# Where seven block products replace eight: heads gain them, two projections lose them

## The chip, the core and the metric

One NeuronCore of a Trainium2 chip runs the whole block as one launch. The metric is the device time of that launch in microseconds (us). The kernel before takes 2250.86 us, median of 3 runs (2249.49 to 2253.15).

## What is computed

One residual block on 256 tokens with D = 2048, 8 retention heads (key width 256, value width 512) and a feed-forward width of 5632, all in float32:

```
h = RMSNorm(x)
[cb|cc|cv | q|k|v|g | gate_conv|gate_ret] = h @ w_in
y_conv = (cb * causal_dwconv3(cc * cv)) @ w_conv_out
y_ret  = (silu(g) * GroupNorm(Retention(rotary q, rotary k, v))) @ w_ret_out
x += (sigmoid(gate_conv) * y_conv + sigmoid(gate_ret) * y_ret) @ w_o
x += SwiGLU(RMSNorm(x))                      # w_ffn_in: 2048 x 11264, w_ffn_out: 5632 x 2048
x += sigmoid(RMSNorm(x) @ w_ple_gate) * (p @ w_ple_proj)
out = RMSNorm(x)
```

## The kernel before, in words

**Split products.** Every float32 operand is written as a high part of type fp32r and the rest, also fp32r. A product of a 128 x 128 stationary block of activations and a 128 x 512 moving block of weights is then three matmuls (hi·hi, hi·lo, lo·hi): `thrice`, lines 227 to 229, and `products`, lines 353 to 355. A chunk of weights comes by DMA into a raw buffer (3 of them, `raw_pool`); ScalarE (ACT) casts it to the high part and VectorE (DVE) subtracts to get the low part (`halves`, lines 333 and 334). These parts lie in `part_pool`, six tiles, so three plain chunks are in flight. Weights stream through once; the 256 tokens are two halves t of 128.

**Two kinds of product.** `project` makes 512 columns of output for both token halves from 16 row blocks of the weights: 96 matmuls into two PSUM banks. `product_group` makes two such column blocks c1 and c2 at once, over 8 pairs of row blocks. A plain pair is a 2 x 2 by 2 x 2 block product with 8 block products, that is 24 matmuls. In a *fast* pair (a table such as `FAST3` says which) seven block products do, 21 matmuls; for these, four sums of the weight blocks are made on DVE (lines 261, 262, 264, 265) with their own casts and low parts (lines 263, 266 and 268), and four sums of the activation blocks, the *stationary forms*, are made once by `further_forms` (lines 208 to 222) for all column blocks that use them. The products of a group run in seven PSUM banks out of eight up to the last fast pair; then DVE joins the banks (lines 293 to 297) and at the end adds what came later (line 302). `FAST3` has fast pairs 1, 3 and 5; `FAST4` has 1, 3, 4 and 6.

**Order of the work.** Heads 0 to 4, each as gate projection g (with its SiLU), q and k together with the rotation on DVE (lines 573 to 587), and v, then scores, values, group norm, and transposes into yrT; then `ret_out(0)` over the first four heads; heads 5 to 7; the convolution's groups `conv_cv` (cc and cv of one column block) and `conv_b` (cb of two), with `ret_out(1)` after the first; four `gate` groups for gate_conv and gate_ret; two groups `co` (w_conv_out) and two groups `wo` (w_o); eleven groups `f` (w_ffn_in), with `fo` (w_ffn_out) woven in from the third on; the embedding gate `pg` and the end. Small steps such as transposes are put off with `later(n, fn)`, which runs fn after n more chunks of weights. All groups from the convolution to w_ffn_in are `product_group`s with FAST3, or FAST4 in w_ffn_in.

**Engines.** Tile pools and a scheduler turn this into one fixed order for each engine, and semaphores keep data apart. On each engine instructions run in that order.

## Time and profile before

| what | value |
|---|---|
| median of 3 runs | 2250.86 us |
| the profiled execution's own time | 2248.99 us |
| its span | 2247.2 us |
| TensorE (PE) busy, matmuls | 2186.1 us, 97%, 9796 matmuls |
| weight loads (PEld) busy | 1781.5 us, 79% |
| DVE busy | 1712.8 us, 76% |
| ACT busy | 1061.1 us, 47% |
| HBM traffic | 190 GB/s over the span |
| mean granted TensorE clock | 0.994 |

A matmul's row in the profile lasts longer than the time to the next one's start, since matmuls are pipelined; how fast PE runs is read from the distance of the starts, or from the number of matmuls in a stretch. The share of DVE differs strongly between stages, so the stages are looked at apart.

### The profile page before, as it was taken

The numbers are of one execution on the slowest core, as the hardware profiler recorded it, in microseconds if no ns is written. First come the engines' busy times: TensorE is split into PE (matmuls) and PEld (weight loads), VectorE is DVE, ScalarE is ACT, GpSimd is POOL, SyncE is SP. The second block draws the span as 40 slices with busy tenths as digits, with TensorE's granted clock in tenths as the row PEclk, the third lists the DMA queues.
The fourth block names the chain that finished last, engine by engine and source line by source line (L and its number), as shares of the span: only waits on it lengthen the run. The fifth ranks groups of instructions, "written<-read, shape, count | busy, mean of one in ns | idle before, by whom it ended". The sixth has DMA issues, their size and how long they took to land.

```text
span 2247.2 us, 25045 instructions
## 1 busy us (share of the span) xinstructions
PE 2186.1 (97%) x9796; PEld 1781.5 (79%) x9796; DVE 1712.8 (76%) x1797; ACT 1061.1 (47%) x967; POOL 9.4 (0%) x19
## 2 busy tenths in 40 slices
...
GB/s 260 187 190 171 181 182 177 218 207 176 184 150 195 253 205 172 161 199 184 224 197 200 197 189 173 150 185 189 225 188 180 175 189 206 187 225 192 187 186 133
DMA packets 235126, 428.47 MB, mean 191 GB/s; under 512 B 11392, under 2 KB 46336, under 8 KB 235008
## 3 DMA queue, kind: packets, MB, share of 16 engines
...
HBM read 420.54 MB, written 6.29 MB: 190 GB/s over the span
## 4 chain that ended last, share of the span: by engine, by line
PE 80%; DVE 10%; ACT 5%; DMA 3%; issue 2%; SPq 0%; ACTq 0%; DVEq 0%; POOLq 0%
PE f_p L228 5%; PE f_p L229 5%; PE f_p L227 5%; PE g_ps L353 3%; PE g_ps L355 3%; PE fo_ps L353 3%; PE fo_ps L355 3%; PE g_ps L354 3%; PE fo_ps L354 3%; PE v_ps L353 3%; PE qk_ps L353 3%; PE v_ps L355 3%; PE v_ps L354 3%; PE ro_ps L227 3%; PE qk_ps L354 3%; PE ro_ps L229 3%
## 5 line engine op out<-in xcount | busy, mean ns | idle before, releaser
L334 DVE TENSOR_TENSOR f_b_lo<-f_raw,f_b_hi 128x2048 fp32r<-128x2048 f32 (+1 forms) x88 | 177.3, 2023 | 61.3 <-ACT f_b_hi L333 61.3
L333 ACT CAST f_b_hi<-f_raw 128x2048 fp32r<-128x2048 f32 (+1 forms) x88 | 148.8, 1693 | 88.3 <-PE fo_ps L354 48.9
L228 PE MATMUL f_p<-f_b_lo,h2T_hi 128*128 128x512 f32 x374 | 146.7, 392 | 1.9 <-DVE f_b_lo L334 1.7
L229 PE MATMUL f_p<-f_b_hi,h2T_lo 128*128 128x512 f32 x374 | 146.0, 390 | 0.0
L227 PE MATMUL f_p<-f_b_hi,h2T_hi 128*128 128x512 f32 x374 | 135.8, 396 | 4.7 <-ACT f_b_hi L333 4.6
L354 PE MATMUL fo_ps<-fo_lo,aT_hi 128*128 128x512 f32 x352 | 138.0, 392 | 0.0
L353 PE MATMUL fo_ps<-fo_hi,aT_hi 128*128 128x512 f32 x352 | 137.2, 394 | 0.0
L355 PE MATMUL fo_ps<-fo_hi,aT_lo 128*128 128x512 f32 x352 | 137.1, 390 | 0.0
L334 DVE TENSOR_TENSOR ro_lo<-ro_raw,ro_hi 128x2048 fp32r<-128x2048 f32 x32 | 73.3, 2291 | 74.7 <-ACT ro_hi L333 74.7
L263 ACT CAST f_t_hi<-f_raw 128x1024 fp32r<-128x1024 f32 x44 | 46.4, 1054 | 167.3 <-DVE f_raw L262 75.5
L334 DVE TENSOR_TENSOR qk_lo<-qk_raw,qk_hi 128x2048 fp32r<-128x2048 f32 x32 | 73.3, 2292 | 60.8 <-ACT qk_hi L333 60.8
L334 DVE TENSOR_TENSOR g_lo<-g_raw,g_hi 128x2048 fp32r<-128x2048 f32 (+1 forms) x36 | 73.9, 2053 | 59.2 <-ACT g_hi L333 59.1
L268 DVE TENSOR_TENSOR f_t_lo<-f_raw,f_t_hi 128x1024 fp32r<-128x1024 f32 x88 | 106.4, 1221 | 16.3 <-ACT f_t_hi L266 8.9
L334 DVE TENSOR_TENSOR v_lo<-v_raw,v_hi 128x2048 fp32r<-128x2048 f32 x32 | 73.3, 2290 | 59.4 <-ACT v_hi L333 59.4
L333 ACT CAST fo_hi<-fo_raw 128x2048 fp32r<-128x2048 f32 x44 | 84.2, 1914 | 68.9 <-PE fo_ps L354 41.0
L333 ACT CAST v_hi<-v_raw 128x2048 fp32r<-128x2048 f32 x32 | 61.2, 1913 | 111.9 <-PE qk_ps L354 86.0
L334 DVE TENSOR_TENSOR fo_lo<-fo_raw,fo_hi 128x2048 fp32r<-128x2048 f32 x44 | 100.6, 2287 | 15.9 <-ACT fo_hi L333 15.9
L333 ACT CAST ro_hi<-ro_raw 128x2048 fp32r<-128x2048 f32 x32 | 61.2, 1912 | 97.7 <-PE ro_ps L228 80.0
L333 ACT CAST qk_hi<-qk_raw 128x2048 fp32r<-128x2048 f32 x32 | 61.1, 1909 | 92.6 <-PE g_ps L354 73.5
L353 PE MATMUL g_ps<-g_hi,hT_hi 128*128 128x512 f32 x256 | 100.7, 395 | 4.2 <-ACT hT_hi L171 4.2
L354 PE MATMUL g_ps<-g_lo,hT_hi 128*128 128x512 f32 x256 | 100.5, 393 | 0.0
L353 PE MATMUL v_ps<-v_hi,hT_hi 128*128 128x512 f32 x256 | 100.5, 393 | 0.0
...
## 6 DMA issues: line engine op xcount, KB each, us to landing
...
```

What stands on the lines that cost most here:

```text
L227: nc.tensor.matmul(out=ps, lhsT=xh, rhs=wh, start=first, stop=False)
L228: nc.tensor.matmul(out=ps, lhsT=xh, rhs=wl, start=False, stop=False)
L229: nc.tensor.matmul(out=ps, lhsT=xl, rhs=wh, start=False, stop=last)
L263: nc.scalar.copy(out=hi[:, 0:2, :], in_=raw[:, 0:2, :])
L268: tt(out=lo[:, js, :], in0=raw[:, js, :], in1=hi[:, js, :].bitcast(F32), op=ALU.subtract)
L333: last_copy[0] = nc.scalar.copy(out=hi[:, :n, :], in_=src)
L334: nc.vector.tensor_tensor(out=lo[:, :n, :], in0=src, in1=hi[:, :n, :].bitcast(F32), op=ALU.subtract)
L353: nc.tensor.matmul(out=ps, lhsT=xh[:, ts], rhs=wh, start=first, stop=False)
L354: nc.tensor.matmul(out=ps, lhsT=xh[:, ts], rhs=wl, start=False, stop=False)
L355: nc.tensor.matmul(out=ps, lhsT=xl[:, ts], rhs=wh, start=False, stop=last)
```

## The change

A second table, `FAST2`, has two fast pairs (1 and 3). Heads 1 to 7 project g and v in one `product_group` with FAST2 instead of two `project`s, after q and k; their scores are made in that group, and the group norm's last step goes from DVE to ACT. The stationary forms of h are asked for in head 0. The convolution's groups use FAST2 instead of FAST3, and the first of them is now a plain group for cb (column blocks 0 and 1). The gate groups keep FAST3. w_conv_out and w_o become plain (`plain_group`, 192 matmuls, four banks), and so their stationary forms go. w_ffn_in uses FAST2 for its first two groups and FAST4 after that; the source of h2's forms is written by ACT from PSUM and not added up on DVE. The matmuls become 9826, the DVE instructions 1692 (1797 before), and ACT's remain 932 in the program.

```diff
+FAST2 = (False, True, False, True, False, False, False, False)
...
             pt = transposed(src, j0, f"{name}_t{j0}")
+            a = form_source(f"{name}_{j0}") if forms is not None and any(forms[1][len(forms[0]) :]) else None
...
+                    if a is not None:
+                        nc.scalar.activation(out=a[:, j, :], in_=pt[:, j, :], func=AF.Copy, scale=g)
+            if forms is not None:
+                further_forms(a, *forms, f"{name}_{j0}")
...
+    def plain_group(lhs, w, k0, c1, c2, name):
+
+        ps = [[bank(f"{name}_ps{c}{t}") for t in range(NT)] for c in range(2)]
+        n = D // P
+        for k in range(0, n, 2):
+            ws = halves(load_pair(w, k0 + k, c1, c2, f"{name}_{k}"), f"{name}_{k}")
+            for j in range(2):
+                xh, xl = lhs[k0 + k + j]
+                for c in range(2):
+                    for t, ts in enumerate((t1, t2)):
+                        thrice(ps[c][t], (xh[:, ts], xl[:, ts]), ws[2 * c + j], k == j == 0, k + j == n - 1)
+            group_done()
+        return ps
...
-        for t in range(NT):
-            nc.vector.tensor_scalar(
-                out=on[:, t, :],
-                in0=o_ps[t],
...
+        for t in range(NT):
+            nc.scalar.activation(
+                out=on[:, t, :], in_=o_ps[t], func=AF.Identity, scale=rstd[:, t : t + 1], bias=shift[:, t : t + 1]
             )
...
+    def head(h):
+        mask = small.tile([P, 3 * P], F32, tag="mask", name=f"mask{h}")
+        nc.sync.dma_start(out=mask, in_=masks[h])
+        ps = project(hT, D // P, [(w_in[0], C_Q + h * DK, DK), (w_in[0], C_K + h * DK, DK)], f"qk{h}")
+        qkT, probs = [], []
+        later(2, partial(turn_qk, h, rope(h, ps), qkT))
+        later(5, partial(attend_early, h, qkT, mask, probs))
+        g, v = product_group(hT, hF, FAST2, w_in[0], C_RG + h * DV, C_RV + h * DV, f"gv{h}")
...
+        on = blk([P, NT, W], F32, f"on{h}")
+        later(1, partial(mix_late, h, probs, vh, vl, on, g))
...
+        later(2, make_hF)
...
-    head(0, first)
+    first_head(0, first)
...
     def conv_cv(n):
-        c, v = product_group(hT, hF, FAST3, w_in[0], C_C + n * W, C_V + n * W, f"cv{n}")
+        c, v = product_group(hT, hF, FAST2, w_in[0], C_C + n * W, C_V + n * W, f"cv{n}")
...
     def conv_b(n):
-        bs = product_group(hT, hF, FAST3, w_in[0], C_B + n * W, C_B + (n + 1) * W, f"cb{n}")
+        bs = product_group(hT, hF, FAST2, w_in[0], C_B + n * W, C_B + (n + 1) * W, f"cb{n}")
...
-    conv_cv(0)
+
+    ps = plain_group(hT, w_in[0], 0, C_B, C_B + W, "cb0")
...
     ret_out(1)
-    conv_cv(1)
-    conv_b(0)
+    for n in range(2):
+        conv_cv(n)
+        later(5, partial(conv_gate, n, first_b[n], ys[n]))
...
-        ms = product_group(ycT, ycF, FAST3, w_conv_out[0], n * W, (n + 1) * W, f"co{n}")
...
+        ps = plain_group(ycT, w_conv_out[0], 0, n * W, (n + 1) * W, f"co{n}")
...
-        xs = product_group(mT, mF, FAST3, w_o[0], n * W, (n + 1) * W, f"wo{n}")
...
+        ps = plain_group(mT, w_o[0], 0, n * W, (n + 1) * W, f"wo{n}")
...
-        a, b = product_group(h2T, h2F, FAST4, w_ffn_in[0], n * W, D_FF + n * W, f"f{n}")
+        a, b = product_group(h2T, h2F, FAST4 if n > 1 else FAST2, w_ffn_in[0], n * W, D_FF + n * W, f"f{n}")
```

How the order moves is shown at three places. Line numbers after the change are those of the new file; `L334` of before is `L351` there, lines 261 to 268 are 278 to 285, line 302 is 319 and lines 227 to 229 are 230 to 232.

**DVE in head 4, from the rotation of q and k on.** `ab` and `qk` belong to the rotation, `_lo` are low parts of weights, and `yrT_lo` those of the head before. Before:

```order
L334 TENSOR_TENSOR v_lo<-v_raw,v_hi 128x2048 x2
L573 SCALAR_TENSOR_TENSOR ab_0_2452<-qk_ps_2325,r_r,rope_sb 128x512 x2
L584 TENSOR_TENSOR qk_2451<-ab_0_2452 128x2x128
L587 TENSOR_TENSOR qk_2451<-ab_0_2452 128x2x128
L573 SCALAR_TENSOR_TENSOR ab_1_2457<-qk_ps_2326,r_r,rope_sb 128x512 x2
L334 TENSOR_TENSOR v_lo<-v_raw,v_hi 128x2048
L584 TENSOR_TENSOR qk_2451<-ab_1_2457 128x2x128
L587 TENSOR_TENSOR qk_2451<-ab_1_2457 128x2x128
```

And now, where the group `gv` of g and v follows:

```order
L351 TENSOR_TENSOR gv_b_lo<-gv_raw_2509,gv_b_hi 128x2048
L562 TENSOR_TENSOR on_2313<-on_2313,gv_ca 128x1024
L351 TENSOR_TENSOR gv_b_lo<-gv_raw_2544,gv_b_hi 128x1536
L278 TENSOR_TENSOR gv_raw_2544<-gv_raw_2544 128x512
L279 TENSOR_TENSOR gv_raw_2544<-gv_raw_2544 128x512
L281 TENSOR_TENSOR gv_raw_2544<-gv_raw_2544 128x512
L174 SCALAR_TENSOR_TENSOR yrT_lo<-yrT_t_2416,gains,yrT_hi 128x256
L598 SCALAR_TENSOR_TENSOR ab_0_2497<-qk_ps_2316,r_r,rope_sb 128x512 x2
L174 SCALAR_TENSOR_TENSOR yrT_lo<-yrT_t_2425,gains,yrT_hi 128x256
L282 TENSOR_TENSOR gv_raw_2544<-gv_raw_2544 128x512
```

The rotation and the yrT low parts now stand among the weight sums of the group's first fast pair (lines 278 to 282), and the multiplication by the gate (`on`) just ahead of them; before, the rotation stood among plain splits, and yrT's low parts some rows earlier.

**PE in head 4, where q and k are transposed.** Before, in the middle of v:

```order
L353 MATMUL v_ps_2463<-v_hi,hT_hi 128x512
L354 MATMUL v_ps_2463<-v_lo,hT_hi 128x512
L355 MATMUL v_ps_2463<-v_hi,hT_lo 128x512
L146 MATMUL qkT_t_2526<-ident,qk_2451 128x128 x4
L146 MATMUL qkT_t_2533<-ident,qk_2451 128x128 x4
L353 MATMUL v_ps_2462<-v_hi,hT_hi 128x512
L354 MATMUL v_ps_2462<-v_lo,hT_hi 128x512
L355 MATMUL v_ps_2462<-v_hi,hT_lo 128x512
```

Now, at the end of gv's first fast pair (`gv_t` are sums of weight blocks, `hF` stationary forms):

```order
L230 MATMUL gv_p_2578<-gv_t_hi,hF_2_s 128x512
L231 MATMUL gv_p_2571<-gv_t_lo,hF_2_s 128x512
L232 MATMUL gv_p_2571<-gv_t_hi,hF_2_s 128x512
L231 MATMUL gv_p_2524<-gv_t_lo,hF_2_s 128x512
L232 MATMUL gv_p_2524<-gv_t_hi,hF_2_s 128x512
L147 MATMUL qkT_t_2587<-ident,qk_2496 128x128 x2
L230 MATMUL gv_p_2516<-gv_b_hi,hT_hi 128x512
L230 MATMUL gv_p_2524<-gv_b_hi,hT_hi 128x512
L230 MATMUL gv_p_2528<-gv_b_hi,hF_0_d 128x512
L231 MATMUL gv_p_2578<-gv_t_lo,hF_2_s 128x512
```

The transposes of one q and k now come in three pieces (2, 2 and 4 matmuls) between the group's products, and not in one piece of eight.

**DVE at the seam from w_o to w_ffn_in.** Before, the last group `wo` is joined among the first weights `f`:

```order
L334 TENSOR_TENSOR f_b_lo<-f_raw_9792,f_b_hi 128x1536
L222 TENSOR_TENSOR h2T_s<-h2T_m,h2T_s 128x512
L294 TENSOR_TENSOR wo_cb<-wo_p_9448,wo_ca 128x512
L261 TENSOR_TENSOR f_raw_9792<-f_raw_9792 128x512
L295 TENSOR_TENSOR wo_ca<-wo_p_9441,wo_cb 128x512
L302 TENSOR_TENSOR wo_ca<-wo_p_9386,wo_ca 128x512
L262 TENSOR_TENSOR f_raw_9792<-f_raw_9792 128x512
L296 TENSOR_TENSOR wo_cb<-wo_p_9394,wo_ca 128x512
L297 TENSOR_TENSOR wo_cb<-wo_p_9394,wo_cb 128x512
L264 TENSOR_TENSOR f_raw_9792<-f_raw_9792 128x512
L302 TENSOR_TENSOR wo_ca<-wo_p_9390,wo_ca 128x512
L302 TENSOR_TENSOR wo_cb<-wo_p_9696,wo_cb 128x512
```

And now:

```order
L351 TENSOR_TENSOR f_b_lo<-f_raw_9809,f_b_hi 128x1536
L222 TENSOR_TENSOR h2T_2_s<-h2T_2_m,h2T_2_s 128x512
L278 TENSOR_TENSOR f_raw_9809<-f_raw_9809 128x512
L810 TENSOR_TENSOR x_2_9719<-wo_ps_9381,x_2_9719 128x512
L810 TENSOR_TENSOR x_2_9719<-wo_ps_9382,x_2_9719 128x512
L279 TENSOR_TENSOR f_raw_9809<-f_raw_9809 128x512
L810 TENSOR_TENSOR x_3_9723<-wo_ps_9383,x_3_9723 128x512
L810 TENSOR_TENSOR x_3_9723<-wo_ps_9384,x_3_9723 128x512
L281 TENSOR_TENSOR f_raw_9809<-f_raw_9809 128x512
```

Of the joining, four additions of the residual from PSUM remain.

## Rows read from the trace of the kernel before

**Rows 1.** The page's busy time, share of the span and instructions of each engine.

```profile
PE 2186.1 (97%) x9796; PEld 1781.5 (79%) x9796; DVE 1712.8 (76%) x1797; ACT 1061.1 (47%) x967; POOL 9.4 (0%) x19
```

**Rows 2.** PE's timeline in head 1: start, duration (us), line, operation, tiles, shapes.

```profile
99.85 0.39 PE L353 MATMUL g_ps<-g_hi,hT_hi 128*128 128x512 f32 x1
...
108.46 0.39 PE L355 MATMUL g_ps<-g_hi,hT_lo 128*128 128x512 f32 x1
108.69 1.03 PE L146 MATMUL yrT_t<-ident,on 128*128 128x128 f32 x8
109.48 0.48 PE L353 MATMUL qk_ps<-qk_hi,hT_hi 128*128 128x512 f32 x1
```

**Rows 3.** Windows: head 2, cv0, ret_out(1), cv1-cb2, gates, co, wo, f0-f2, f3.

```profile
core 0: us, PE busy (x) PEld busy (x) DVE busy (x) ACT busy (x) POOL busy (x), PEclk, DMA share, GB/s
109.48:180.13 70.65, 70.65 (x329) 58.87 (x327) 42.92 (x44) 28.35 (x24) 0.69 (x1) 1.00 0.56 182
...
668.55:717.37 48.82, 44.75 (x192) 34.57 (x191) 41.44 (x53) 25.56 (x26) 0.00 (x0) 1.00 0.45 152
717.37:805.30 87.93, 87.93 (x393) 72.92 (x392) 49.19 (x40) 34.09 (x24) 0.00 (x0) 1.00 0.72 238
805.30:1029.51 224.21, 217.43 (x956) 174.38 (x955) 198.90 (x216) 118.74 (x108) 0.00 (x0) 1.00 0.55 188
1029.51:1202.32 172.81, 170.79 (x749) 137.81 (x748) 156.93 (x160) 94.64 (x84) 0.00 (x0) 1.00 0.61 209
1202.32:1294.11 91.79, 88.45 (x383) 69.25 (x382) 85.57 (x100) 46.67 (x43) 0.00 (x0) 1.00 0.53 180
1294.11:1395.18 101.07, 92.70 (x400) 72.98 (x398) 93.14 (x112) 50.50 (x57) 0.00 (x0) 0.97 0.57 196
1395.18:1567.06 171.88, 159.26 (x678) 123.48 (x677) 160.34 (x188) 86.92 (x86) 0.69 (x1) 0.98 0.50 172
1567.06:1632.22 65.16, 64.33 (x285) 52.37 (x284) 56.00 (x55) 31.74 (x25) 0.00 (x0) 1.00 0.58 194
```

**Rows 4.** Groups by line, DVE: line, operation, tiles, shapes, count, busy us, mean ns, idle before.

```profile
L334 DVE TENSOR_TENSOR gate_b_lo<-gate_raw,gate_b_hi 128x2048 fp32r<-128x2048 f32 x20 | 45.8, 2288 | 5.0 <-ACT gate_b_hi L333 5.0
...
L268 DVE TENSOR_TENSOR gate_t_lo<-gate_raw,gate_t_hi 128x1024 fp32r<-128x1024 f32 x24 | 29.0, 1220 | 4.6 <-PE gate_p L229 3.1 <-ACT gate_t_hi L263 1.5
...
L573 DVE SCALAR_TENSOR_TENSOR ab<-qk_ps,r_r,rope_sb 128x512 f32<-128x512 f32 x32 | 22.5, 745 | 5.0 <-PE qk_ps L355 5.0
...
L334 DVE TENSOR_TENSOR gate_b_lo<-gate_raw,gate_b_hi 128x1536 fp32r<-128x1536 f32 x12 | 21.0, 1753 | 0.0
...
L302 DVE TENSOR_TENSOR f_ca<-f_p,f_ca 128x512 f32<-128x512 f32 x22 | 15.0, 683 | 0.0
...
L172 DVE SCALAR_TENSOR_TENSOR yrT_lo<-yrT_t,gains,yrT_hi 128x256 fp32r<-128x256 f32 x32 | 14.0, 477 | 0.3 <-ACT yrT_hi L171 0.2
...
L524 DVE TENSOR_SCALAR on<-o,stats,rstd 128x512 f32<-128x512 f32 x16 | 12.2, 806 | 0.3
...
L546 DVE TENSOR_TENSOR on<-on,sg 128x1024 f32<-128x1024 f32 x8 | 9.8, 1225 | 0.2
...
L262 DVE TENSOR_TENSOR gate_raw<-gate_raw 128x512 f32<-128x512 f32 x12 | 8.3, 692 | 0.3
...
L584 DVE TENSOR_TENSOR qk<-ab 128x256 f32<-128x256 f32 x16 | 6.8, 422 | 0.2
```

**Rows 5.** The chain that ended last, the longest pieces within 1290 to 1400 us: start, us, what.

```profile
1334.62 7.16 DMA wo_raw<-in_w_o_dram
...
1357.37 7.75 DMA wo_raw<-in_w_o_dram
```

**Rows 6.** Waits over the span: who waited for whom, us in total, times, longest us.

```profile
ACT v_hi L333 <- PE qk_ps L354: 86.0, 24, 5.6
```

**Rows 7.** PE's timeline in the group cb0: the transposes of u.

```profile
856.77 0.60 PE L146 MATMUL uT<-ident,cv_cb 128*128 128x128 f32 x4
...
862.25 0.60 PE L146 MATMUL uT<-ident,cv_cb 128*128 128x128 f32 x4
```

165 lines of the change are left out of this document (90 added, 75 removed).

## The prediction

> **What bounds the kernel now.** The page comes first: PE's matmuls are busy 97% of the span, DVE 76%, ACT 47% [rows 1]. That looks like a kernel that only fewer matmuls can shorten. PE's timeline says what full speed is: from 99.85 to 108.46 us lie 38 starts, 0.2266 us each, though one row lasts 0.39 us; eight transposes take the 0.79 us up to the next product, 0.1 us each [rows 2]. With this the stages are gone through by windows [rows 3]. In each I take the matmuls that the program has there, multiply, and call the rest of the window its **loss**:
>
> - A head (70.65 us) has no idle PE, PEld 83% of the time and DVE 61%: loss 0. ret_out(1), plain: 384 x 0.2266 + 0.8 = 87.8 of 87.93, loss 0.1, DVE 56%.
> - cv0: 183 matmuls and 8 transposes, 42.3 of 48.82: loss 6.5.
> - cv1, cb0, cv2, cv3, cb2: 915 and 40, 211.3 of 224.21: loss 12.9, DVE 89%.
> - Four gate groups: 732 and 16, 167.5 of 172.81: loss 5.3, DVE 91%.
> - co: 366 and 16, 84.5 of 91.79: loss 7.3, DVE 93%.
> - wo: 366 and 32, 86.1 of 101.07: loss 14.9, DVE 92%.
> - f0 to f2 with the first fo: 636 and 40, 148.1 of 171.88: loss 23.7, DVE 93%.
> - f3 with its fo, the pattern that then repeats: 276 and 8, 63.3 of 65.16: loss 1.8, DVE 86%.
>
> So PE is the bound where DVE is under about 61%, loses 2.8% at 86%, and up to 15% at 92 to 93%, where DVE works on weight sums, low parts and stationary forms at once. The six stages before f3 lose 6.5 + 12.9 + 5.3 + 7.3 + 14.9 + 23.7 = 70.6 us. PE's granted clock is 0.97 in wo and 0.98 in f0 to f2 [rows 3]: short stretches at the lower level, 1.2 GHz, after idle PE; their cost is in these losses.
>
> How much is to be had hangs on this reading. By idle time of the matmul row alone the six stages give only 4.1 + 6.8 + 2.0 + 3.3 + 8.4 + 12.6 = 37.2 us. PEld decides: in the head it is 58.87/70.65 = 83.3%; in f0 to f2 it is 123.48 us, which at 83.3% take 148.2 of the 171.88, a loss of 23.7 [rows 3], as counted. The two readings give a change of -34.2 and of -9.8 us below. The Trainium skill, Perfetto Trace Analysis, section Identifying the Most-Contended Engine, takes a side between these rows: matmul busy time is a poor measure of headroom and LDWEIGHTS busy time a good one; by it the -34.2 stands.
>
> **The change part by part.**
>
> *Matmuls.* Each fast pair saves three. Before, 14 FAST3 groups and 11 FAST4 groups have 42 + 44 = 86; now gv has 7 x 2, cv and cb 5 x 2, gates 4 x 3, f 2 x 2 + 9 x 4, 76 in all. The 30 more matmuls cost 30 x 0.2266 = **+6.8**. The transposes stay as many.
>
> *Heads 1 to 7.* g and v lose 8 low parts of 2.29 and get 6 of 2.29 and 2 of 1.75 (-1.1), 8 weight sums of 0.69 (+5.5), 4 low parts of sums of 1.22 (+4.9) and 8 joins of 0.68 (+5.5); two group-norm steps of 0.81 go to ACT (-1.6) [rows 4]. DVE gets 13.2 us more: 42.9 + 13.2 = 56.1 of 70.65 - 6 x 0.2266 = 69.3, 81%. Between the head now (61%, 0) and f3 (86%, 2.8%) that is 2.2%, 1.5 us a head. Bounds: 0 as in ret_out(1), and 6.5 as in cv0, the dearest FAST3 group. I take 1.5, since f3 is the nearest row: **+10.5**. Both norm steps on ACT, 47% busy, hide.
>
> *cv0's place.* A plain group for cb stands there, like ret_out(1): loss 0.2, so **-6.3**. The loss of cv0 does not pass to the next group as long as h's forms are made in head 0; DVE made them there already.
>
> *The five groups with FAST2.* A plain pair for a fast one saves DVE 4 x 0.69 + 2 x 1.22 - (2.29 - 1.75) = 4.7 us [rows 4]: 39.8 to 35.1 a group, against PE's 186 x 0.2266 + 0.8 = 42.9, 82%. By the same line 1.0 a group: 12.9 to 5, **-7.9**. Bounds: nothing, or all 12.9.
>
> *Gates.* Same table: 0, bounds ±2 from the forms of ycT that are no longer made in gate3.
>
> *co and wo, plain.* DVE has 8 x 2.29 = 18.3 us of splits and a few joins in a group of 192 x 0.2266 = 43.5: under 60%, as in ret_out(1). Loss 0.1 each, and 1 for the seams: 22.2 to 1.2, **-21.0**. Bounds: down to 0, up to 15, if the transfers that stand in the chain there, 7.16 and 7.75 us [rows 5], are late on their own account.
>
> *f0 to f2.* At the start DVE no longer carries wo's joins (order of the seam), f0 and f1 have two fast pairs, and the sums of h2's blocks come from ACT. But the second half of h2 and three forms that only f2 uses are still made in f0. Three groups at f3's 1.8 and 2.0 for that: 23.7 to 7.4, **-16.3**. Bounds: 5 and 15.
>
> *After f2* nothing changes.
>
> Sum: 6.8 + 10.5 - 6.3 - 7.9 - 21.0 - 16.3 = -34.2. The profiled execution took 2248.99 (span 2247.2), 1.9 under the median of 2250.86; 2248.99 - 34.2 = **2214.8**, and I say 2215.
>
> **The rivals.**
>
> *DVE falls behind at the start of gv (slower).* From gv's first low part to the low parts of the second fast pair's sums DVE has: 2 x 2.29 + 2 x 1.75 low parts, 8 sums of 0.69, 4 x 1.22, the rotation 4 x 0.745 + 4 x 0.42, yrT 4 x 0.48, the gate 1.23, one qkT 0.68: 27.0 us [rows 4]. PE gets to these products after 78 matmuls and 8 transposes, 18.5 us. If DVE had no lead, each head would wait 8.5 us: 7 x 8.5 = 59.5 for my 10.5, 2215 + 49 = **2264**. It decides from 7.0 us a head on, a lead under 1.5 us: there the loss passes 10.5 + 34.2 and the 0.2% of 4.5. Against it: now the casts wait for PE to free the part tiles, 86.0 us in 24 waits before v alone [rows 6], so splits run up to three chunks (16 us) ahead, and most of the first 7 us of this list can be done in q and k's time; the rotation and yrT (6.6 us) cannot. And the dearest FAST3 group, cv0, loses 6.5. Chance 5%.
>
> *PSUM banks run short in the heads.* gv holds seven of eight banks where g and v held two, so q's and k's transposes go through the last one, and a piece waits until the low part of the piece before is read. If PE stood still meanwhile, each head would lose what lies between two such pieces in cb0, 5.5 us [rows 7]: 7 x 5.5 = 38.5, **2253**, no change. Against it: in cb0, with seven banks as well, products fill those 5.5 us, and cv1 to cb2 lose 2.6 a group with everything; the order of PE in gv puts products between the pieces too. 3%. The Trainium skill, Perfetto Trace Analysis, section Optimizing Tensor Performance, Matmuls, speaks against the change here: groups of matmuls should rotate through different PSUM banks so that one is emptied while the next runs, and by that rule the sum would be 2253. No row here shows a wait for a bank by itself.
>
> *Transfers bound wo and f, not DVE.* Then plain products wait for the same weights: of the 37.3 us from co, wo and f0 to f2 some 15 (its two longest pieces there, 7.16 + 7.75 us [rows 5]) stay: **2230**. For it: the chain. Against it: ret_out(1) reads 238 GB/s and loses 0.1, wo 196 GB/s [rows 3]; a raw buffer is free only when DVE is through with it, so a late transfer is late DVE. 10%.
>
> *The matmul row was right*: only 37.2 us are lost and the gains shrink to 37.2/70.6 of 51.5 less the same 17.3: 2249 - 27.1 + 17.3 = **2239**. 5%.
>
> *Heads lose nothing* and f starts at 5: 2215 - 10.5 - 2.4 = **2202**. 10%.
>
> That the change doesn't do what it says is out: the order has 9826 matmuls and 1692 DVE instructions.
>
> **How the numbers follow.** Forecast 67%, and the rivals as said; about 0.2%, 4.5 us, is what a measurement of this kernel can tell from no change. The likeliest case gives 2215. The range takes in free heads (2202) and late transfers (2230), and upward the bound of heads at 3 us (+10.5) with five groups as they are (+7.9), downward that of f0 to f2 at 5 beside free heads: 2200 to 2237. Left out are the two cases of dear heads, the matmul-row case and the outer bounds. Faster: 67 + 10 + 5 + 10, less 1 for heads at 6 us, 91%; the same: the banks and that one, 4%; slower 5%.
>
> **What would show it.** Right: heads of 69 to 71 us, DVE near 80% there, and PE idle under 2 us at gv's fast pairs; co and wo near 88 us each with DVE under 60% and a clock of 1.00; the stretch from f0 to f3's start 16 us shorter than 171.88; f3 still 65.2. Wrong: heads over 75 us, with PE waiting for `gv_t_lo` (DVE late) or for `qkT_t` (banks); casts in wo waiting for `wo_raw`'s transfers.

## The result: 2200.0 us, and where the 50 us went

The changed kernel takes 2200.03 us (median of 4 runs, 2197.04 to 2201.09), the kernel before 2250.24 beside it: a ratio of 0.9772, 95% interval 0.9755 to 0.9789. The forecast was 2215, with a range from 2200 to 2237. The direction and the order of size were right. The time lies on the range's lower edge, with two of the four runs below it, and the change gave about 50 us where 35 were forecast. The profiled span went from 2247.2 to 2198.2 us.

The page of the changed kernel answers to [rows 1]. Below its busy times stand the shares of the chain that ended last, of the changed kernel first and then of the kernel before:

```profile
PE 2169.9 (99%) x9826; PEld 1787.4 (81%) x9826; DVE 1651.3 (75%) x1692; ACT 1062.8 (48%) x967; POOL 9.4 (0%) x19
...
PE 92%; DVE 4%; ACT 2%; issue 1%; DMA 1%; SPq 0%; ACTq 0%; POOLq 0%; DVEq 0%
...
PE 80%; DVE 10%; ACT 5%; DMA 3%; issue 2%; SPq 0%; ACTq 0%; DVEq 0%; POOLq 0%
```

The matmul row hardly shows the gain: 97% became 99%. The chain does: PE holds 92% of it where it held 80%.

The windows by stage answer to [rows 3]: head (gv of head 2 and qk of head 3), ret_out(1), cv0 to cb2, gates, co, wo, f0 to f2, f4 with its fo:

```profile
core 0: us, PE busy (x) PEld busy (x) DVE busy (x) ACT busy (x) POOL busy (x), PEclk, DMA share, GB/s
179.22:248.70 69.48, 69.48 (x321) 57.63 (x320) 55.21 (x64) 33.76 (x31) 0.69 (x1) 1.00 0.56 185
704.81:791.85 87.04, 87.04 (x385) 72.07 (x384) 40.70 (x24) 30.86 (x18) 0.00 (x0) 1.00 0.69 229
791.85:1010.92 219.07, 217.50 (x979) 179.06 (x978) 180.54 (x192) 113.82 (x103) 0.00 (x0) 1.00 0.58 197
1010.92:1181.95 171.03, 170.21 (x749) 138.19 (x748) 150.48 (x145) 93.15 (x80) 0.00 (x0) 1.00 0.59 202
1181.95:1270.81 88.86, 88.86 (x402) 73.75 (x401) 49.70 (x34) 34.92 (x25) 0.00 (x0) 1.00 0.61 204
1270.81:1361.49 90.68, 90.68 (x418) 75.40 (x417) 53.18 (x52) 42.78 (x48) 0.00 (x0) 1.00 0.63 206
1361.49:1519.12 157.63, 154.39 (x690) 124.92 (x688) 136.39 (x152) 83.02 (x84) 0.69 (x1) 1.00 0.55 188
1584.44:1649.90 65.46, 64.38 (x286) 52.36 (x284) 56.00 (x55) 31.72 (x25) 0.00 (x0) 1.00 0.57 193
```

With 0.2266 us a matmul and 0.1 a transpose, as in the prediction, the losses are now: head 0.2 (six matmuls fewer than 70.65 would be 69.29), the five groups 219.07 - 214.7 = 4.3, gates 3.5, co 0.3, wo 0.5, f0 to f2 157.63 - 150.8 = 6.8. The first row is the surprise: DVE is busy 55.21/69.48 = 79% of a head, near the forecast 81%, and PE's row has no idle time at all. The last row is much as before, 2.1 us lost at 86% (f3 before: 1.8).

PE's waits of the changed kernel by what they waited for (us in total, times, longest us):

```profile
PE f_p L230 <- ACT f_b_hi L350: 4.1, 11, 0.6
PE aT_t L147 <- DVE f_ca L833: 3.2, 8, 0.5
PE f_p L231 <- DVE f_t_lo L285: 2.3, 9, 0.7
...
PE cv_p L231 <- DVE cv_b_lo L351: 1.2, 1, 1.2
```

Three of the four stand in w_ffn_in, 8 to 11 times each: at its one place where two fast pairs follow each other (3 and 4), and at the transposes. None of 0.2 us or more names a `gv` tile.

### The profile page after: what moved, and what is told of

The parts are those of the page before. It is cut to its first block, busy times and chain, and to the rows that moved or that the text cites. A ratio compares the mean times of both kernels' runs of the same rounds, so it can differ in the third digit from the quotient of the medians.

```text
span 2198.2 us, 25135 instructions
## 1 busy us (share of the span) xinstructions
PE 2169.9 (99%) x9826; PEld 1787.4 (81%) x9826; DVE 1651.3 (75%) x1692; ACT 1062.8 (48%) x967; POOL 9.4 (0%) x19
## 3 DMA queue, kind: packets, MB, share of 16 engines
q8 instruction: 77, 1.26, 0.2%
## 4 chain that ended last, share of the span: by engine, by line
PE 92%; DVE 4%; ACT 2%; issue 1%; DMA 1%; SPq 0%; ACTq 0%; POOLq 0%; DVEq 0%
PE f_p L231 6%; PE f_p L232 6%; PE f_p L230 6%; PE gv_p L230 4%; PE gv_p L231 4%; PE gv_p L232 4%; PE fo_ps L370 3%; PE fo_ps L372 3%; PE fo_ps L371 3%; PE qk_ps L372 3%; PE qk_ps L370 3%; PE qk_ps L371 3%; PE ro_ps L232 3%; PE ro_ps L230 3%; PE ro_ps L231 3%; PE cv_p L231 2%
## 5 line engine op out<-in xcount | busy, mean ns | idle before, releaser
L351 DVE TENSOR_TENSOR f_b_lo<-f_raw,f_b_hi 128x2048 fp32r<-128x2048 f32 (+1 forms) x88 | 179.2, 2046 | 66.7 <-ACT f_b_hi L350 66.7
L231 PE MATMUL f_p<-f_b_lo,h2T_hi 128*128 128x512 f32 x402 | 157.1, 391 | 0.5 <-DVE f_b_lo L351 0.5
L232 PE MATMUL f_p<-f_b_hi,h2T_lo 128*128 128x512 f32 x402 | 156.5, 390 | 0.0
L350 ACT CAST gv_b_hi<-gv_raw 128x2048 fp32r<-128x2048 f32 (+1 forms) x56 | 101.0, 1805 | 101.6 <-PE qk_ps L371 45.4
L351 DVE TENSOR_TENSOR gv_b_lo<-gv_raw,gv_b_hi 128x2048 fp32r<-128x2048 f32 (+1 forms) x56 | 120.1, 2154 | 34.6 <-ACT gv_b_hi L350 34.6
L351 DVE TENSOR_TENSOR ro_lo<-ro_raw,ro_hi 128x2048 fp32r<-128x2048 f32 x32 | 73.4, 2293 | 88.5 <-ACT ro_hi L350 88.5
L231 PE MATMUL gv_p<-gv_b_lo,hT_hi 128*128 128x512 f32 x336 | 131.0, 390 | 0.0
L232 PE MATMUL gv_p<-gv_b_hi,hT_lo 128*128 128x512 f32 x336 | 130.8, 389 | 0.0
L230 PE MATMUL gv_p<-gv_b_hi,hT_hi 128*128 128x512 f32 x336 | 126.8, 393 | 0.0
L351 DVE TENSOR_TENSOR qk_lo<-qk_raw,qk_hi 128x2048 fp32r<-128x2048 f32 x32 | 73.3, 2291 | 58.5 <-ACT qk_hi L350 58.5
L351 DVE TENSOR_TENSOR fo_lo<-fo_raw,fo_hi 128x2048 fp32r<-128x2048 f32 x44 | 100.6, 2286 | 14.8 <-ACT fo_hi L350 14.8
L285 DVE TENSOR_TENSOR f_t_lo<-f_raw,f_t_hi 128x1024 fp32r<-128x1024 f32 x80 | 96.7, 1221 | 16.1 <-ACT f_t_hi L283 8.9
L371 PE MATMUL qk_ps<-qk_lo,hT_hi 128*128 128x512 f32 x256 | 100.3, 392 | 0.0
L372 PE MATMUL qk_ps<-qk_hi,hT_lo 128*128 128x512 f32 x256 | 99.8, 390 | 0.0
```

Source lines behind the costliest of these rows:

```text
L230: nc.tensor.matmul(out=ps, lhsT=xh, rhs=wh, start=first, stop=False)
L231: nc.tensor.matmul(out=ps, lhsT=xh, rhs=wl, start=False, stop=False)
L232: nc.tensor.matmul(out=ps, lhsT=xl, rhs=wh, start=False, stop=last)
L285: tt(out=lo[:, js, :], in0=raw[:, js, :], in1=hi[:, js, :].bitcast(F32), op=ALU.subtract)
L350: last_copy[0] = nc.scalar.copy(out=hi[:, :n, :], in_=src)
L351: nc.vector.tensor_tensor(out=lo[:, :n, :], in0=src, in1=hi[:, :n, :].bitcast(F32), op=ALU.subtract)
```

## The experiments

Two theories were set against each other. **Share theory**, that of the prediction: PE's loss rises with DVE's share of a stage. **Local theory**: PE loses only where DVE's work on a few chunks in a row is more than PE's time for them and more than the lead that the buffers allow. A fast pair takes DVE 1.75 + 4 x 0.69 + 2 x 1.22 = 6.95 us [rows 4] and PE 21 x 0.2266 = 4.8; a plain one 2.29 and 5.4.

This table gives the runs, stage by stage, from the start of the first product of a stage to that of the next (us; worked out from the traces; "heads" from the second of head 1's products on and with ret_out(0), "conv" with ret_out(1), "f3 on" up to the embedding gate). Each row is one profiled execution. Between the rows with six part tiles, stages whose program a run leaves as it is still differ: gates by up to 1.9 us, f0 to f2 by 2.4, f3 on by 1.4, so smaller differences there say little.

| run | median | ratio to before, 95% | heads | conv | gates | co | wo | f0 to f2 | f3 on |
|---|---|---|---|---|---|---|---|---|---|
| before | 2250.24 | | 559.07 | 360.96 | 172.81 | 91.79 | 101.07 | 171.88 | 570.78 |
| changed | 2200.03 | 0.9755 to 0.9789 | 548.56 | 352.70 | 171.03 | 88.86 | 90.68 | 157.63 | 569.33 |
| heads0 | 2208.98 | 0.9795 to 0.9822 | 556.47 | 354.16 | 170.19 | 88.85 | 90.68 | 156.60 | 569.85 |
| heads3 | 2196.39 | 0.9741 to 0.9768 | 543.72 | 352.73 | 170.60 | 88.85 | 90.68 | 156.76 | 570.41 |
| seam8 | 2208.27 | 0.9793 to 0.9820 | 552.29 | 357.23 | 169.92 | 88.86 | 90.68 | 157.83 | 569.68 |
| seam16 | 2211.47 | 0.9807 to 0.9834 | 556.66 | 357.23 | 169.99 | 88.85 | 90.68 | 157.52 | 569.20 |
| even | 2200.38 | 0.9758 to 0.9788 | 548.56 | 352.74 | 171.61 | 91.29 | 86.13 | 159.99 | 570.41 |
| lumpy12 | 2227.20 | 0.9877 to 0.9906 | 548.56 | 352.74 | 171.78 | 103.88 | 100.98 | 160.14 | 570.03 |
| lumpy | 2249.94 | 0.9982 to 1.0001 | 548.55 | 352.75 | 169.92 | 113.47 | 119.13 | 155.57 | 569.66 |
| adj | 2228.48 | 0.9882 to 0.9915 | 562.88 | 361.69 | 177.50 | 88.86 | 90.68 | 157.20 | 570.23 |
| alt | 2184.01 | 0.9689 to 0.9717 | 548.56 | 352.70 | 170.38 | 88.86 | 90.68 | 158.54 | 554.91 |
| cowo | 2224.85 | 0.9866 to 0.9899 | 558.98 | 355.91 | 171.25 | 88.84 | 90.64 | 167.49 | 571.11 |
| f01 | 2211.20 | 0.9804 to 0.9833 | 548.56 | 352.68 | 170.06 | 88.85 | 90.68 | 167.69 | 569.00 |
| lumpy_p6 | 2250.70 | 0.9983 to 1.0001 | 548.55 | 352.70 | 170.41 | 114.71 | 119.57 | 155.41 | 569.96 |
| lumpy_p8 | 2215.46 | 0.9822 to 0.9850 | 548.38 | 350.16 | 167.87 | 104.93 | 108.77 | 152.41 | 562.42 |
| adj_p8 | 2188.99 | 0.9703 to 0.9731 | 548.45 | 350.13 | 174.51 | 88.85 | 90.68 | 152.42 | 564.67 |
| best | 2184.43 | 0.9682 to 0.9710 | 543.71 | 355.48 | 173.02 | 88.86 | 90.68 | 156.73 | 554.90 |
| heads_p8 | 2190.55 | 0.9719 to 0.9746 | 543.59 | 350.20 | 169.01 | 88.86 | 90.68 | 161.84 | 565.35 |
| all_p8 | 2196.49 | 0.9745 to 0.9771 | 543.60 | 352.67 | 171.03 | 88.86 | 90.68 | 161.56 | 568.68 |
| f01_p8 | 2201.86 | 0.9763 to 0.9789 | 543.59 | 352.84 | 172.17 | 88.85 | 90.68 | 160.11 | 574.78 |

### Share or run: co and wo with DVE's work put back

After the change co and wo are plain, with DVE busy under 60%. DVE work was put back there in three shapes, 24 instructions in each of the four groups, ahead of low parts (they add zero times another row, so the values stay):

```diff
-    def halves(src, name):
+    def halves(src, name, extra=0):
...
+        for _ in range(extra):
+            nc.vector.scalar_tensor_tensor(
+                out=src[:, 0, :], in0=src[:, 1, :], scalar=0.0, in1=src[:, 0, :], op0=ALU.mult, op1=ALU.add
+            )
...
+            extra = (3) if name[:2] in ("co", "wo") else 0                       # even
+            extra = (12 if k in (4, 12) else 0) if name[:2] in ("co", "wo") else 0   # lumpy12
+            extra = (24 if k == 8 else 0) if name[:2] in ("co", "wo") else 0         # lumpy
```

> The changed kernel, with three more DVE instructions (128x512, estimated at 0.69 us each from the weight sums) ahead of each low part in the plain groups co and wo: 32 chunks of w_conv_out and w_o get 2.1 us each. DVE's share there goes to about (49.7 + 33)/88.9 = 93% in co and (53.2 + 33)/90.7 = 95% in wo, what it was before the change; the matmuls stay. Share theory (PE's loss rises with DVE's share of a stage): co and wo lose 7.3 and 14.9 us again, 2222 us. Local theory (PE loses only where DVE's work on a few chunks in a row is more than PE's time for them and more than the lead of three chunks that the buffers allow): each chunk now takes DVE 2.29 + 2.07 = 4.4 us and PE 24 x 0.2266 = 5.4 us, so nothing is lost but at the seams, 2200 to 2204 us, co and wo together within 183 us.

> As in the run with the work spread evenly, the same 24 additional DVE instructions in each of the four plain groups, but 12 of them ahead of the low part of the third chunk and 12 ahead of that of the seventh, of eight. Share theory: as with even work, 2222 us. Local theory: such a chunk takes DVE 12 x 0.69 + 2.29 = 10.6 us, about two chunks of PE (10.9 us); with two to three chunks (10.9 to 16.3 us) in hand PE waits 0 to 2 us at each of the eight places: 2200 to 2210 us.

> The same 24 additional DVE instructions in each of the four plain groups, all ahead of the low part of the fifth chunk of eight. Share theory: as with even work, 2222 us. Local theory: that chunk takes DVE 24 x 0.69 + 2.29 = 18.9 us; with two chunks in hand (10.9 us) PE waits 8 us, with three (16.3 us) 2.6 us, four times: 10 to 32 us, 2210 to 2232 us, and the wait stands in one piece at the fifth chunk's second matmul, with the other chunks undisturbed.

Even: 2200.38 us, no loss. The windows of co and wo in that run:

```profile
1181.88:1273.17 91.29, 89.51 (x402) 73.57 (x400) 83.06 (x84) 34.64 (x24) 0.00 (x0) 1.00 0.60 197
1273.17:1359.30 86.13, 86.13 (x397) 71.63 (x396) 78.97 (x93) 42.69 (x48) 0.00 (x0) 1.00 0.62 207
```

DVE is busy 83.06/91.29 = 91% in co and 92% in wo, close to the 93% and 92% at which these stages lost 7.3 and 14.9 us before [rows 3]; together they now take 177.4 us. (A part of wo's tail slips behind f0's first products, so co, wo and f0 to f2 are to be added: 337.4 us, against 337.2 without the work.) **Share theory falls here**: nearly the same share, and the 22 us of loss are not there.

The same work in lumps costs 27 and 50 us. So the local theory holds in kind, but its size was off: lumpy12 was to take 2200 to 2210 us, and lumpy came out above its 2232. Lumpy's timeline at the first lump shows why: DVE, then ACT, then PE (start, duration, line, operation, tiles, and in brackets the idle time before and what ended it):

```profile
1192.87 17.41 DVE L353 SCALAR_TENSOR_TENSOR co_raw<-co_raw 128x512 f32<-128x512 f32 x24 [3.10 <-ACT co_hi L351]
1210.37 4.49 DVE L356 TENSOR_TENSOR co_lo<-co_raw,co_hi 128x2048 fp32r<-128x2048 f32 x2
...
1190.92 1.91 ACT L351 CAST co_hi<-co_raw 128x2048 fp32r<-128x2048 f32 x1 [3.48 <-PE co_ps L231]
1196.36 1.91 ACT L351 CAST co_hi<-co_raw 128x2048 fp32r<-128x2048 f32 x1 [3.53 <-PE co_ps L231]
1201.80 1.91 ACT L351 CAST co_hi<-co_raw 128x2048 fp32r<-128x2048 f32 x1 [3.53 <-PE co_ps L231]
...
1201.83 1.07 PE L230 MATMUL co_ps<-co_hi,ych 128*128 128x512 f32 x4
1212.71 0.79 PE L231 MATMUL co_ps<-co_lo,ych 128*128 128x512 f32 x1 [9.81 <-DVE co_lo L356]
1213.30 0.63 PE L232 MATMUL co_ps<-co_hi,ycl 128*128 128x512 f32 x1
```

The casts come every 5.44 us, one chunk of PE, and each waits for a product of PE: a cast needs part tiles, and these come free when PE is through the chunk three before. So DVE can start on a chunk only 1.95 us (the cast) after that, when two chunks lie ready. PE then has 2 x 5.44 - 1.95 = 8.9 us, and the high products of the late chunk itself (four matmuls, 0.9 us): **a lead of 9.8 us, not of three chunks, 16.3**. DVE needs 17.50 + 2.29 = 19.8 us from its start at 1192.87 on; PE waits 9.8 to 10 us. Three of the run's four waits cost 9.97 us each; the fourth, in wo's last group, costs 13.25. lumpy12 agrees where a lump stands alone: DVE needs 8.78 + 2.29 = 11.1 us for the second lump of co's two groups and wo's first, 1.3 more than the lead, and the measured losses are 1.26, 1.25 and 1.26 us. The first lump of each group, where DVE also finishes the stage before, loses 3.0 to 4.0, which the expectation had not counted.

The 9.8 us hold for plain chunks. A fast pair takes four of the six part tiles, two for its blocks and two for their sums, so fewer chunks can lie ready there; no run measured that lead.

The rest of a lump's price is the clock: behind the wait of 9.8 us the granted clock is 0.50, the 1.2 GHz level, for 4.4 us, and then full:

```profile
1212.71:1217.14 4.43, 4.43 (x10) 3.47 (x11) 4.35 (x2) 0.00 (x0) 0.00 (x0) 0.50 0.72 228
1217.38:1222.00 4.62, 4.62 (x22) 3.81 (x21) 0.59 (x1) 1.91 (x1) 0.00 (x0) 1.00 0.91 303
```

Ten matmuls start in the first stretch and 22 in the second of like length; at full clock ten take 2.3 us, so the slow stretch costs 2.2.

### Two fast pairs in a row

The same matmuls and the same DVE instructions, only the table differs. adj sets pairs in a row in the stages where they alternated, alt takes them apart in w_ffn_in, the one place where the change has two in a row:

```diff
# adj
-FAST3 = (False, True, False, True, False, True, False, False)
-FAST2 = (False, True, False, True, False, False, False, False)
+FAST3 = (False, True, True, False, False, True, False, False)
+FAST2 = (False, True, True, False, False, False, False, False)
# alt (f0 and f1 take the first two of these)
-FAST4 = (False, True, False, True, True, False, True, False)
+FAST4 = (True, False, True, False, True, False, True, False)
```

> The changed kernel, with fast pairs 1 and 2 in a row in place of 1 and 3 in the heads and the convolution, and 1, 2 and 5 in place of 1, 3 and 5 in the gates; w_ffn_in stays. Matmuls, DVE instructions and so DVE's share of each stage stay the same. Share theory: 2200 us, within 2. Local theory: two fast pairs in a row take DVE 2 x 6.95 = 13.9 us and PE 2 x 21 x 0.2266 = 9.5 us; the period of f3, which has such a pair in a row (3 and 4), loses 1.8 us, of which 0.9 lies just behind that pair. 7 heads, 5 groups of the convolution and 4 gates lose 0.5 to 1.0 us more each: 2208 to 2216 us.

> The changed kernel with the fast pairs of w_ffn_in at 0, 2, 4 and 6 in place of 1, 3, 4 and 6 (f0 and f1: 0 and 2 in place of 1 and 3), so that no two stand in a row. Matmuls and DVE instructions stay. Share theory: 2200 us, within 2. Local theory: the 0.9 us behind the pair in a row goes in nine periods: 2192 us; a fast pair at the start of a group stands nearer to the joins of the group before, which may give back a part: 2192 to 2198 us.

adj: 2228.48 us, 28 more, in the heads (+14.3), the convolution (+9.0) and the gates (+6.5), more than was expected. alt: 2184.01 us, 16 less, better than expected: f3 on fell by 14.4 us, nearly all that these periods lost. Both waits of these periods are gone with it, the one behind the pairs in a row and the one at the transposes, so their shares are not told apart. One period of alt (f4 with its fo), where [rows 3] has 65.16 for f3's:

```profile
1581.59:1645.12 63.53, 63.53 (x286) 52.59 (x284) 56.60 (x55) 32.17 (x25) 0.00 (x0) 1.00 0.60 199
```

DVE's share is 89%, higher than before, and PE's row has no idle time. In adj's third gate group DVE stands so, and PE's two waits with it (start, duration, line, tiles):

```profile
1126.29 1.22 DVE L286 TENSOR_TENSOR gate_t_lo<-gate_raw,gate_t_hi 128x1024 fp32r<-128x1024 f32 x1
1127.43 0.69 DVE L283 TENSOR_TENSOR gate_raw<-gate_raw 128x512 f32<-128x512 f32 x1
1128.03 1.75 DVE L352 TENSOR_TENSOR gate_b_lo<-gate_raw,gate_b_hi 128x1536 fp32r<-128x1536 f32 x1
1129.70 1.22 DVE L286 TENSOR_TENSOR gate_t_lo<-gate_raw,gate_t_hi 128x1024 fp32r<-128x1024 f32 x1
1130.83 0.69 DVE L279 TENSOR_TENSOR gate_raw<-gate_raw 128x512 f32<-128x512 f32 x1
...
1133.62 1.22 DVE L286 TENSOR_TENSOR gate_t_lo<-gate_raw,gate_t_hi 128x1024 fp32r<-128x1024 f32 x1
1135.22 2.29 DVE L352 TENSOR_TENSOR gate_b_lo<-gate_raw,gate_b_hi 128x2048 fp32r<-128x2048 f32 x1 [0.39 <-ACT gate_b_hi L351]
...
1133.43 0.73 PE L231 MATMUL gate_p<-gate_t_hi,hF_s 128*128 128x512 f32 x2 [0.75 <-ACT gate_t_hi L281]
1134.89 0.50 PE L232 MATMUL gate_p<-gate_t_lo,hF_s 128*128 128x512 f32 x1 [0.73 <-DVE gate_t_lo L286]
```

DVE works without a break from one pair's low parts to the other's, and among PE's waits of that run are `gv_t_lo`, `gv_b_lo`, `cv_t_lo` and `gate_t_lo`.

### What sets the lead

A run of work that outruns the lead should cost less where the lead is longer. Two more part tiles (8 KB a partition each) were bought with four block tiles (4 KB each); p6 has fewer block tiles alone.

```diff
-NBLK = 30
+NBLK = 26
...
-    part_pool = ctx.enter_context(tc.tile_pool(name="part", bufs=6))
+    part_pool = ctx.enter_context(tc.tile_pool(name="part", bufs=8))   # p8 alone
```

> The run with 24 additional DVE instructions on the fifth chunk of each group of co and wo, with 26 block tiles for 30 and the same six part tiles: the control for the next run. co and wo together 232.6 us as with 30 block tiles, within 3; other stages may be slower where block tiles run short.

> As the control, 26 block tiles, but eight part tiles for six: four plain chunks in flight. There the cast of a chunk waits for PE to be through the chunk three before it; with eight tiles, four before. If part tiles set the lead, it grows by one chunk, 5.44 us: each of the four waits of about 9.8 us falls to about 4.4, and what PE loses at the lower clock behind it falls or goes: co and wo together 232.6 - 4 x 5.4 to 4 x 7.5, 202 to 211 us. If the three raw buffers set it, the waits stay within 1 us of the control's.

> The run with two fast pairs in a row in heads, convolution and gates, with 26 block tiles for 30 and eight part tiles for six. If the loss behind two such pairs is DVE's run of work against the lead (13.9 us against PE's 9.5 and what lies ready), a lead longer by some 5 us takes most of it: heads to ret_out(1) from +14, gates from +6.5 us against the changed kernel to under a third of that. If it is DVE's throughput over the group, whatever the lead, it stays.

The control is as lumpy, co and wo 234.3 us. With eight tiles they take 213.7, 20.6 less, a little above the expected 202 to 211: the four losses at the waits went from 9.97, 9.97, 9.97 and 13.25 us to 6.59, 5.04, 5.05 and 7.85, by 4.7 each on average for a chunk of 5.44, and the slow matmuls behind them stay in part. Two of PE's four waits of lumpy_p8, where lumpy has 9.81 at the first:

```profile
1204.29 0.79 PE L231 MATMUL co_ps<-co_lo,ych 128*128 128x512 f32 x1 [6.43 <-DVE co_lo L356]
...
1257.36 0.68 PE L231 MATMUL co_ps<-co_lo,ych 128*128 128x512 f32 x1 [4.88 <-DVE co_lo L356]
```

**So the part tiles set the lead, and not the raw buffers.**

adj_p8: 2188.99 us, 39 less than adj. To price its pairs in a row, it is set against lumpy_p8, which has the same tiles and outside co and wo the changed kernel's program: heads 548.45 against 548.38, convolution 350.13 against 350.16, gates 174.51 against 167.87. **With eight part tiles pairs in a row cost nothing in the heads and the convolution; with six they outran the lead there.** In the gates they still cost 6.6 us, as with six tiles (6.5), where under a third of that was expected. There the local theory has no answer yet. PE's waits stand in the last two of the four gate groups alone, and why DVE is late in these two is open.

The longer lead pays in the changed kernel's own program, too: in the stages outside co and wo lumpy_p8 is 15.8 us shorter than its control, 7.5 of it from f3 on. By that estimate the changed kernel with eight part tiles would come close to alt, but no run has that alone.

### The heads

heads0 gives heads 1 to 7 plain projections again (g, then q and k, then v); heads3 gives g and v three fast pairs; seam8 and seam16 add 8 and 16 instructions after the rotation:

```diff
# heads3
-        g, v = product_group(hT, hF, FAST2, w_in[0], C_RG + h * DV, C_RV + h * DV, f"gv{h}")
+        g, v = product_group(hT, hF, FAST3, w_in[0], C_RG + h * DV, C_RV + h * DV, f"gv{h}")
# seam8 (seam16: 16), at the end of rope
+        if h > 0:
+            extra(qk, 8)    # 8 times out=x, in0=qk[:, 0, :], in1=qk[:, 1, :], op=ALU.add; x is read by nobody
```

> The changed kernel with heads 1 to 7 as before the change: g, q and k, v as plain projections, and scores after v; the group norm's last step stays on ACT, the rest as changed. 42 matmuls more, +9.5 us, and what the heads now lose is gone. The prediction's terms (heads' fast pairs save 9.5 and lose 10.5): 2199 us. The windows of the changed kernel (69.48 us a head against 70.65): 2200 + 7 x 1.17 = 2208 us.

> The changed kernel with three fast pairs (1, 3, 5) in the group of g and v of heads 1 to 7. 21 matmuls fewer, -4.8 us; DVE gets 4.7 us more in each head, 55.2 + 4.7 = 59.9 of 68.8 us, 87%. Share theory, by the line of the prediction (61% loses nothing, 86% loses 2.8%): 2.9%, 2.0 us a head, 14 us in all: 2200 - 4.8 + 14 - 2 (what the heads lose now) = 2207 us. Local theory: fast and plain pairs still alternate, nothing is lost: 2195 to 2197 us.

> The changed kernel with eight more DVE instructions (128x512, 0.69 us each) after the rotation in each of heads 1 to 7; their results go nowhere, and in DVE's order they stand among the work of the first fast pair of g and v: 5.5 us more just where the rival 'DVE late at the start of gv' put its 27.0 us against PE's 18.5. Share theory: DVE (55.2 + 5.5)/69.5 = 87%, 2 us a head: 2212 to 2215 us. Local theory: DVE is then 27.0 + 5.5 - 18.5 = 14 us short there, less than the lead of three chunks (16.3 us): 2200 to 2203 us. If the lead is only just enough now (8.5 us): 7 x 5.5 = 39 more, 2239 us.

> As the run with eight more DVE instructions in each head, with sixteen: 11.0 us more. Share theory: DVE (55.2 + 11)/69.5 = 95%, where co to f2 of before lost 8 to 15%: 5 to 10 us a head, 2235 to 2270 us. Local theory: 27.0 + 11.0 - 18.5 = 19.5 us short against a lead of three chunks, 16.3 us: 3 us a head, 2221 us; less if part of the sixteen slips behind the fast pair in DVE's order. A lead that is only just enough now: 7 x 11 = 77, 2277 us.

heads0: 2208.98 us, the 2208 that the windows gave: the fast pairs in the heads are worth 9 us, nearly all of their 42 matmuls, and not -1. heads3: 2196.39 us, where the local theory had 2195 to 2197 and share theory 2207; its heads take 543.72 us, which is 4.84 less for 21 matmuls of 4.76. One of its heads:

```profile
176.22:244.98 68.76, 68.76 (x319) 57.08 (x318) 59.51 (x69) 34.91 (x33) 0.69 (x1) 1.00 0.57 187
```

DVE is busy 59.51/68.76 = 87%, and a head loses 0.2 us. The additional work in gv costs 8.3 us for 7 x 5.5 and 12.6 for 7 x 11.0 (heads and convolution together, since head 7's end slips into the latter): 1.2 and 1.8 us a head. Share theory's 12 to 15 and 35 to 70 are out. The local theory's 0 to 3 was too low for seam8 and its 21 too high for seam16. The trace of seam8 shows that the added work does not stand where the expectation put it (DVE and PE in head 2):

```profile
186.50 1.22 DVE L285 TENSOR_TENSOR gv_t_lo<-gv_raw,gv_t_hi 128x1024 fp32r<-128x1024 f32 x1
...
190.50 0.69 DVE L597 TENSOR_TENSOR extra<-qk 128x512 f32<-128x512 f32 x1
...
199.92 2.30 DVE L351 TENSOR_TENSOR gv_b_lo<-gv_raw,gv_b_hi 128x2048 fp32r<-128x2048 f32 x1
...
202.27 0.50 PE L231 MATMUL gv_p<-gv_b_lo,hT_hi 128*128 128x512 f32 x1 [0.63 <-DVE gv_b_lo L351]
```

The first added instruction starts behind the last low part of the first fast pair's sums. Six of the eight stand ahead of the low part at 199.92, for which PE then waits; in seam16 six of the sixteen do. So these two runs did not put work ahead of the first fast pair, and the rival "DVE late at the start of gv" is answered by the changed kernel's own heads alone, where PE waits for no `gv` tile; the 39 and 77 us of a lead that is only just enough are not tested by them.

### One part alone: co and wo in the kernel before, and f0 and f1

cowo is the kernel before with `plain_group` for co and wo and without their stationary forms; f01 gives f0 and f1 of the changed kernel four fast pairs again.

```diff
# cowo (and "wo" in the same way; turn_m makes no forms, the calls for ycF go)
-        ms = product_group(ycT, ycF, FAST3, w_conv_out[0], n * W, (n + 1) * W, f"co{n}")
+        ps = plain_group(ycT, w_conv_out[0], 0, n * W, (n + 1) * W, f"co{n}")
# f01
-        a, b = product_group(h2T, h2F, FAST4 if n > 1 else FAST2, w_ffn_in[0], n * W, D_FF + n * W, f"f{n}")
+        a, b = product_group(h2T, h2F, FAST4, w_ffn_in[0], n * W, D_FF + n * W, f"f{n}")
```

> The kernel before with one part of the change alone: w_conv_out and w_o plain, and no stationary forms of their inputs. 36 matmuls more, +8.2 us. The prediction's term: losses of 7.3 + 14.9 us go to 1.2, -21.0; so 2250 - 12.8 = 2237 us, with f0 to f2 at 171.88 us as before. If the joins of the last wo and the late start that it hands on are what slows f0, f0 to f2 get shorter too, by up to 5 us: 2232 us. If transfers bound wo, plain products wait for the same weights: 2250 + 8.2 - 7 = 2251 us.

> The changed kernel with four fast pairs in f0 and f1 too, as before the change. 12 matmuls fewer, -2.7 us. The prediction gave f0 to f2 -16.3 us for three things together: the joins of wo that are gone, the two fast pairs, the source of the forms from ACT. If the two fast pairs carry a third or more of it, 2200 - 2.7 + 5 to 10 = 2202 to 2207 us. If the others carry it, 2197 to 2199 us.

cowo: 2224.85 us, below all three expected times, and twice the gain that the term gave. co and wo fell by 2.95 and 10.43, 13.4 against the 12.8 of the term; the rest came elsewhere: convolution 5.0, gates 1.6, f0 to f2 4.4. The trace of before shows where the 5 us were. On DVE in cv2:

```profile
907.02 0.69 DVE L208 TENSOR_TENSOR ycF_a<-ych,ycl 128x512 f32<-128x512 f32 x1
909.75 0.42 DVE L219 TENSOR_TENSOR ycF_m<-ycF_a 128x256 f32<-128x256 f32 x1
916.47 0.42 DVE L222 TENSOR_TENSOR ycF_d<-ycF_m,ycF_d 128x256 fp32r<-128x256 f32 x1
```

The forms for co, asked for behind the gates, are made in the convolution, 300 us ahead of their use; without them cv2 and cv3 are 5.1 us shorter. f01: 2211.20 us, above the expected 2202 to 2207; f0 to f2 take 10.1 us longer with 2.7 us of matmuls less, so the two fast pairs less in each of f0 and f1 are worth 12.8 us of loss.

### Putting it together

best is alt with three fast pairs in the heads and, again, in the convolution. heads_p8, all_p8 and f01_p8 have eight part tiles and 26 block tiles: alt with heads3, then three fast pairs in the convolution too, then four in f0 and f1.

```diff
# best, all_p8
-        c, v = product_group(hT, hF, FAST2, w_in[0], C_C + n * W, C_V + n * W, f"cv{n}")
+        c, v = product_group(hT, hF, FAST3, w_in[0], C_C + n * W, C_V + n * W, f"cv{n}")
...
-        bs = product_group(hT, hF, FAST2, w_in[0], C_B + n * W, C_B + (n + 1) * W, f"cb{n}")
+        bs = product_group(hT, hF, FAST3, w_in[0], C_B + n * W, C_B + (n + 1) * W, f"cb{n}")
```

> The changed kernel with w_ffn_in's fast pairs at 0, 2, 4, 6 (f0, f1: 0, 2), three fast pairs in the heads' g and v, and three again in the five groups of the convolution: wherever fast and plain pairs alternate. 36 matmuls fewer than in the run with 0, 2, 4, 6 alone. Local theory: 2184 - 4.8 for the heads - 3.4 for the convolution, of which the tighter groups (in the run with w_conv_out and w_o alone plain they lost 0.4 to 1.1 us each) give back 1 to 2: 2176 to 2179 us. Share theory: heads at 87% and the convolution at 89% lose 14 and 7 us: 2195 us or more.

> The run with w_ffn_in's fast pairs at 0, 2, 4, 6 and, besides, three fast pairs in the heads, with 26 block tiles for 30 and eight part tiles for six; the convolution keeps two fast pairs. From 2184: -4.8 for the heads' matmuls; with the longer lead the convolution -2.5, gates -3, f0 to f2 -5 (as in the other runs with eight part tiles): 2168 to 2172 us.

> As heads_p8, with three fast pairs in the five groups of the convolution too: 15 matmuls fewer, -3.4 us. If the loss there was the short lead, convolution and ret_out(1) take 350.1 - 3.4 = 346.7 us, within 1, and the run is 2.5 to 3.4 us under heads_p8. If it was DVE's throughput over the group, the 6.2 us of loss stay: it is 2 to 3 us over heads_p8.

> As all_p8, with four fast pairs in f0 and f1 too: 12 matmuls fewer, -2.7 us. If the loss of f0 to f2 was the short lead, 2 to 3 us under all_p8; if it was throughput (joins, forms, sums and splits of f0 on a DVE that is busy over 90% there), 5 to 10 us over it.

best: 2184.43 us, no better than alt. The heads keep their 4.8 us; the convolution takes 2.8 more for 3.4 us of matmuls less, and the gates 2.6 more. So alternating is not enough there, and 2176 to 2179 were expected. all_p8 against heads_p8 says that the third pair there does not pay with a longer lead either: +2.5 us in the convolution, +2.0 in the gates. f01_p8 against all_p8 is 1.5 us shorter in f0 to f2, where f01 was 10 longer. But f01 had pairs 3 and 4 in a row there and f01_p8 has none, so lead and table are not told apart, and as a whole f01_p8 is 5.4 us slower, by what f3 on lost (6.1).

The three as a whole missed; heads_p8 took 2190.55 us where 2168 to 2172 were expected. Its convolution gained what was expected (-2.5 against alt), the gates half of it (-1.4), but f0 to f2 lost 3.3 and f3 on 10.4. PE's waits of heads_p8:

```profile
PE aT_t L148 <- DVE f_ca L834: 13.4, 9, 4.7
```

alt has no such wait over 0.2 us. With eight tiles and this table PE waits for the SwiGLU product `f_ca`, in all_p8 14.8 and in f01_p8 14.2 us. That DVE now takes splits that became possible earlier ahead of it fits, but the scheduler's order and the block tiles changed along, and with the changed kernel's table eight tiles made f3 on shorter (lumpy_p8). So this is argued, not shown. **alt, another table of fast pairs for w_ffn_in, is the fastest kernel of the study**, with best beside it.

## Why the prediction was off

Point by point, in the prediction's own steps:

- *What bounds the kernel.* Right in kind: matmuls at 0.2266 us plus losses made by DVE, and losses from windows, not from the matmul row's idle time. The rival that the matmul row was right (2239) is out. The Trainium skill, Perfetto Trace Analysis, section Identifying the Most-Contended Engine, judges TensorE's headroom by LDWEIGHTS busy time and not by matmul busy time; the trace agrees: PEld's 124.92 us in f0 to f2, at the head's 83.3%, take 150.0 us of 157.63, a loss of 7.7 where the count gives 6.8.
- *Heads 1 to 7, +10.5: the step that failed.* The interpolation "between the head now (61%, 0) and f3 (86%, 2.8%)" took DVE's share for the cause. Measured are 0.2 us a head, 1.3 in all; that is 9.2 of the 14.8 us by which the span (-49.0) beat the sum (-34.2). The rest is spread over gates, ret_out(0), f3 on and the others, none over 2 us. DVE's work was about right, 12.3 us more a head (42.92 to 55.21) for 13.2. What the runs showed in its place: PE waits where a run of DVE's work outruns the lead, whatever the share. With 79% a head loses 0.2 us, heads3 with 87% loses 0.2 as well, and adj, with the same work and two fast pairs in a row, 2 us a head more. f3 was the nearest row by share, but its 1.8 us come with what no head has, two fast pairs in a row and the wait at aT's transposes, and alt loses 0.2 us at a share of 89%.
- *cv0's place, -6.3:* cb's plain group takes 46.59 us with 201 matmuls and 8 transposes, 46.3 at full rate: right.
- *Gates, 0:* 1.8 less, inside the ±2 named.
- *The five groups, -7.9:* measured 12.9 to 4.3, -8.6. The size came out, but partly by luck: it was read off the same line as the heads, and 5 us of cv2's and cv3's loss were the forms of ycT made there, as cowo shows. The prediction looked for these in the gates. That leaves some 3.5 us for the fast pairs.
- *co and wo, -21.0:* 0.8 us of loss left, -21.4. Right, and the clock is back at 1.00.
- *f0 to f2, -16.3:* -16.9. Of this the two fast pairs less carry 12.8 (f01), and what wo no longer hands on 4.4 (cowo); together 17.2, if the two add up. The forms' source on ACT was not tried alone.
- *After f2, nothing:* -1.4, which is what rows with the same program differ by.
- *The rival of DVE late at the start of gv:* PE waits for no `gv` tile, so its 8.5 us of shortfall were covered. The lead that was to cover them was put too high, at three chunks (16 us), where co and wo show 9.8; that the heads have as much is not shown.
- *The rival of transfers:* co and wo move 204 and 206 GB/s, PE waits for none there, and the casts for 0.2 us.
- *The rival of banks:* in the heads a group holds seven of eight and PE's row has no idle time. The Trainium skill, Perfetto Trace Analysis, section Optimizing Tensor Performance, Matmuls, wants independent groups to rotate through different banks so that one is emptied while the next runs. The changed kernel shows no wait of PE for that of 0.2 us or more; alt and best show one each, 1.6 us in f0 to f2 for the join that empties a bank (`f_ca`).
- *The rival that heads lose nothing*, at 10%, gave 2202 and was the case that came.
